# One ring of weight tiles for all stages, and the additions after a down pass in two groups

## The chip, the cores and the metric

The kernel runs on one core of a Trainium2 chip. The metric is the device time of one execution in microseconds; the median of three runs is what is compared.

## The reference

A decoder trunk of two layers over a sequence of 512 tokens of width 1024, in float32. Each layer is a token mixer followed by a gated feed-forward block with a causal convolution of width 3; every part reads an RMS-normed input and adds its result to the residual stream.

```
for i in range(2):
    h = rms_norm(x, norm_mix[i])
    x = x + (mixer_a(h, ...) if i == 0 else mixer_b(h, ...))
    h = rms_norm(x, norm_ffn[i])
    up = causal_dwconv(h @ w_up, conv_w, conv_b)      # 1024 -> 6144
    gate, val = jnp.split(up, 2, axis=-1)
    x = x + (gelu(gate) * val) @ w_down               # 3072 -> 1024
return rms_norm(x, norm_final)
```

Mixer A projects to 4096, mixes tokens in chunks of 128 and projects back; mixer B projects to 3072, convolves, runs a linear recurrence and projects back.

## The kernel before

**Numbers as pairs.** Activations lie transposed, features on the partitions, 128 to a tile. Every float32 operand of a matmul is kept as a high part and a low part of a faster type (`hi`, `lo`). For a weight chunk, `split` (line 94) makes them: ACT casts the raw chunk to `hi` (line 98) and DVE subtracts to get `lo` (line 99). Three matmuls, hi·hi, hi·lo and lo·hi, stand for one product.

**Weight chunks.** `load` (line 102) issues the DMA of a raw chunk of 128x1024 on SP's queue and then splits it. `block` (line 115) is the plain projection: per chunk of weights it does 24 matmuls of 512 columns into four PSUM banks, and at given chunks it calls hooks; `norm_stat` and `norm_spread` (lines 228 and 235) are such hooks, which turn the sum of squares `acc` into the factor of the norm by a few matmuls (`st`, `rb`).

**Stages.** The kernel has four stages: mixer A, the feed-forward of layer 0, mixer B, the feed-forward of layer 1. `enter` opens the pools of a stage and their memory is used again by the next. The tiles of raw, high and low weights come from the pool `wp` of the stage: three of each tag in the mixers, four high and four low ones in `conv_ffn` (line 522), where raw has three (line 103).

**End of a mixer.** `project` (line 257) multiplies by the output weights in two halves of four banks (`aop`, `bop` in the rows). For each of its banks it adds to the residual tile `xs[k]` (line 262), makes the normed input `xh`, `xl` of the next stage (line 209) and squares for the next norm (line 214).

**Feed-forward.** `up` (line 529) makes 256 gate and 256 value features at a time in 12 calls (`q`), each a `block` of four chunks (`fu`), followed by a scaling, the convolution, the GELU and the product. The down projection is written as a Strassen product with seven terms in `seven` (line 504): per `q`, `weight_sums` (line 469) makes two pairs of high and low parts, a and b, with three sums on DVE, two casts on ACT and two subtractions on DVE; then come 42 matmuls of 256 columns into seven banks, 18 with part a and 24 with part b. `down` (line 561) does this for two halves `m` of the outputs over six `q`. In the rows, `d000`, `d001` are the two halves of the first pass, `d060`, `d061` those of the second, `d100`, `d101` those of layer 1. The last part of layer 1 is a plain projection.

**After each half of a down pass** the seven banks are added to the residual (lines 567 to 580): one copy on ACT and eleven additions on DVE, all at high priority, seven of them with a PSUM operand:

```
nc.vector.tensor_tensor(x2[:, :, t1], x2[:, :, t1], banks[5], op=ALU.subtract)
nc.vector.tensor_tensor(x1[:, :, t1], banks[5], x1[:, :, t1], op=ALU.add)
nc.vector.tensor_tensor(x1[:, :, t1], banks[3], x1[:, :, t1], op=ALU.add)
```

`next_norm` (line 584) then makes the normed input of mixer B in the second pass of layer 0.

**What sets the order.** A scheduler orders each engine's instructions by priority and by when it believes their operands and memory free; splits and additions at `HIGH` go first. Each engine then runs its list strictly in order, and an instruction that waits holds up those behind it. A weight tile is free for its next use when the last matmul on it has ended.

Of the kernel before, what the change touches and what calls it, by code (L numbers as in the profile page):

```python
# [8 lines left out]
F32 = mybir.dt.float32  # L9
BF16 = mybir.dt.bfloat16  # L10
F32R = mybir.dt.float32r
AF = mybir.ActivationFunctionType
ALU = mybir.AluOpType

P = 128
S = 512
# [4 lines left out]
AG = 8  # L21
# [23 lines left out]
def trunk(ctx: ExitStack, tc: tile.TileContext, xT, vecs, a_w_in, a_w_sT, a_b_s, a_w_out,  # L45
          b_w_in, b_w_a, b_w_x, b_w_out, f_w_up, f_w_down, out):
    nc = tc.nc

    const = ctx.enter_context(tc.tile_pool(name="const", bufs=1))
    pp = ctx.enter_context(tc.tile_pool(name="pp", bufs=8, space=bass.MemoryType.PSUM))  # L50

    def psum(name="ps"):
# [39 lines left out]


    def split(raw, shape, name):
        hi = phase["wp"].tile(shape, F32R, tag="hi", name=f"{name}h")
        lo = phase["wp"].tile(shape, F32R, tag="lo", name=f"{name}l")
        with tc.high_priority(HIGH):
            nc.scalar.copy(hi, raw)
            nc.vector.tensor_tensor(lo, raw, hi.bitcast(F32), op=ALU.subtract)
        return hi, lo  # L100

    def load(shape, parts, name):
        raw = phase["wp"].tile(shape, F32, tag="raw", name=f"{name}r", bufs=3)
        for sl, src in parts:
            nc.sync.dma_start(sl(raw), src)
        return split(raw, shape, name)
# [39 lines left out]
    def load_x(k):  # L146
        nc.sync.dma_start(xs[k], xT[k * P:(k + 1) * P, :])

    mixer = enter(("wp", 3), ("yp", 24), ("wk", 7), ("bs", 1))
    bs = phase["bs"].tile([P, AG, P], F32, name="bs")  # L150


# [191 lines left out]
    wv = a_w_in.rearrange("(k p) n -> p k n", p=P)  # L344

    def first_chunk(kc, src):
        raw, hi, lo = (phase["wp"].tile([P, 2, 512], dt, tag=t, name=f"av0{kc}{t}") for t, dt in (("raw", F32), ("hi", F32R), ("lo", F32R)))
        for i in range(2):
            k = 2 * kc + i
            load_x(k)  # L350
            nc.sync.dma_start(raw[:, i], src[:, i])
            with tc.high_priority(HIGH):
                norm_input(k, g0[:, k:k + 1])
                nc.scalar.copy(hi[:, i], raw[:, i])
                nc.vector.tensor_tensor(lo[:, i], raw[:, i], hi[:, i].bitcast(F32), op=ALU.subtract)
        return hi, lo
# [43 lines left out]
            vparts[c, fb] = (h, l)  # L400


    wsr = phase["wp"].tile([P, AG, P], F32, tag="raw", name="wsr")
    nc.sync.dma_start(wsr, a_w_sT.rearrange("g s t -> s g t"))
    wsparts = []
    for i in range(AG // 2):
# [60 lines left out]


    def weight_sums(src, name):
        raw = phase["wp"].tile([P, 4, 256], F32, tag="raw", name=f"{name}r", bufs=3)  # L470
        for k in range(2):
            nc.sync.dma_start(raw[:, 2 * k:2 * k + 2], src[:, k])
        sums = phase["sm"].tile([P, 4, 256], F32, tag="sm", name=f"{name}s")
        parts = []
        with tc.high_priority(HIGH):
            nc.vector.tensor_tensor(sums[:, 0:2], raw[:, 1:3], raw[:, 0:1].broadcast_to([P, 2, 256]), op=ALU.add)
            nc.vector.tensor_tensor(sums[:, 2], raw[:, 1], sums[:, 1], op=ALU.add)
            nc.vector.tensor_tensor(sums[:, 3], raw[:, 3], sums[:, 2], op=ALU.add)
            for t, src in (("a", raw[:, 1:4]), ("b", sums)):
                n = src.shape[1]  # L480
                hi, lo = (phase["wp"].tile([P, n, 256], F32R, tag=g, name=f"{name}{t}{g}", padded_shape=[P, 4, 256]) for g in ("hi", "lo"))
                nc.scalar.copy(hi, src)
                nc.vector.tensor_tensor(lo, src, hi.bitcast(F32), op=ALU.subtract)
                parts.append((hi, lo))
        return parts
# [29 lines left out]
                                         stop=last and j == 1 and m == 2, skip_group_check=True)  # L515
        return banks

    def etile(name):
        return phase["wk"].tile([P, 2, HS], F32, tag="w", name=name)

    def conv_ffn(l, gain_name, gain_off, chunks):
        stack = enter(("wp", 4), ("y", 6), ("yr", 1), ("sm", 1), ("wk", 5))
        wu = f_w_up[l].rearrange("(k p) (two n) -> p k two n", p=P, two=2)
        wd = f_w_down[l].rearrange("(k p) (two n) -> p k two n", p=P, two=2)
        ys, plain = {}, []
        summed = NF // 2 if gain_name else NF // 4


        def up(q):
            def ld(kc):  # L530
                hi, lo = load([P, 2, 2, 256], [
                    (lambda t, h=h: t[:, :, h, :], wu[:, 2 * kc:2 * kc + 2, h, q * 256:(q + 1) * 256]) for h in range(2)
                ], f"fu{l}{q}{kc}")
                return hi.rearrange("p k h n -> p k (h n)"), lo.rearrange("p k h n -> p k (h n)")
            pss = block(KD, ld, xparts, f"f{q}", norm_hooks if q == 0 else {}, chunks)
            y = phase["y"].tile([P, 7, S], F32R, tag="y", name=f"y{q}")
            if q < summed:
                raw = phase["yr"].tile([P, 8, HS], F32, tag="yr", name=f"yr{q}")
            for j in range(2):
                ts = []  # L540
                for half in range(2):
                    f = half * NF + 2 * q + j
                    upt = work("up")
                    nc.vector.tensor_tensor(upt, pss[2 * half + j], rbc, op=ALU.mult)  # L544
                    t = work("cv")
                    conv(t, upt, 3, "f_conv_w", "f_conv_b", l * 6 * NF + f, 2 * NF, l * 2 * NF + f)
                    ts.append(t)
                nc.scalar.activation(ts[0], ts[0], AF.Gelu_apprx_tanh)  # L548
                if q < summed:
                    nc.vector.tensor_tensor(places(raw)[j], halves(ts[0]), halves(ts[1]), op=ALU.mult)  # L550
                else:
                    nc.vector.tensor_tensor(ts[1], ts[0], ts[1], op=ALU.mult)  # L552
                    h, lo = y[:, 2 * j], y[:, 2 * j + 1]
                    nc.scalar.copy(h, ts[1])  # L554
                    nc.vector.tensor_tensor(lo, ts[1], h.bitcast(F32), op=ALU.subtract)
                    plain.append((h, lo))
            if q < summed:
                input_sums(raw, y)
                ys[q] = y

        def down(qs, then):
            for m in range(2):
                banks = seven([(q, ys[q]) for q in qs],
                              lambda q: wd[:, 2 * q:2 * q + 2, :, m * 256:(m + 1) * 256], f"d{l}{qs[0]}{m}")
                x2, x1 = xall[:, 2 * m:2 * m + 2, :], xall[:, 4 + 2 * m:6 + 2 * m, :]
                t0, t1 = slice(0, HS), slice(HS, S)
                with tc.high_priority(HIGH):
                    e1, u2, u3 = (etile(f"d{qs[0]}{m}{t}") for t in ("e1", "u2", "u3"))
                    nc.scalar.copy(e1, banks[1])
                    nc.vector.tensor_tensor(x1[:, :, t0], banks[2], x1[:, :, t0], op=ALU.add)  # L570
                    nc.vector.tensor_tensor(x2[:, :, t0], x2[:, :, t0], banks[4], op=ALU.subtract)
                    nc.vector.tensor_tensor(u2, banks[6], e1, op=ALU.subtract)
                    nc.vector.tensor_tensor(u3, u2, banks[7], op=ALU.subtract)
                    nc.vector.tensor_tensor(x2[:, :, t1], x2[:, :, t1], banks[5], op=ALU.subtract)
                    nc.vector.tensor_tensor(x1[:, :, t1], banks[5], x1[:, :, t1], op=ALU.add)
                    nc.vector.tensor_tensor(x1[:, :, t1], banks[3], x1[:, :, t1], op=ALU.add)
                    for t in (t0, t1):
                        nc.vector.tensor_tensor(x2[:, :, t], x2[:, :, t], u3, op=ALU.add)
                    nc.vector.tensor_tensor(x1[:, :, t0], x1[:, :, t0], e1, op=ALU.add)
                    nc.vector.tensor_tensor(x1[:, :, t1], x1[:, :, t1], u2, op=ALU.subtract)  # L580
                if then:
                    then(m)

        def next_norm(m):
            for k in (2 * m, 2 * m + 1, 4 + 2 * m, 5 + 2 * m):
                norm_input(k, col(gain_name, gain_off + k))
                square(k)

        half = NF // 4
        for q in range(half + 1):  # L590
            up(q)
        down(list(range(half)), None)
        for q in range(half + 1, NF // 2):
            up(q)
        if gain_name:
            down(list(range(half, NF // 2)), next_norm)
        else:
            project_out(NF // 2, f_w_down[l][half * 256:, :], plain, f"fd{l}")
        stack.close()

    mixer.close()
    conv_ffn(0, "norm_mix", KD, None)
    mixer = enter(("wp", 3), ("yp", 24), ("wk", 7))
    log_sigmoid()


# [145 lines left out]
```

## Time and profile before

| | |
|---|---|
| median of 3 runs | 1365.67 us (1365.33 to 1366.09) |
| the profiled execution | 1364.13 us, of which the span is 1362.4 us |
| granted TensorE clock, mean | 0.989 |
| PE busy | 1327.4 us, 97% of the span |
| DVE, ACT busy | 956.7 us (70%), 591.0 us (43%) |
| DMA | 129.30 MB, mean 95 GB/s |

Times in rows are microseconds from the start of the span. In a timeline row the columns are start, length, engine, line, operation, output<-inputs, shape and count; in square brackets stand the idle time ahead of it and what ended it. A matmul's length is modelled and runs over the start of the next one; start to start is what counts. In a row of windows the columns are the stretch, its length, the busy time and the number of instructions of each of PE, PEld, DVE, ACT and POOL, the granted clock as a share of full speed, the share of DMA time and GB/s. A row of waits has the engine and line that waited, for what, the total in us, how many times, and the longest.

### The profile page before, as it was taken

The numbers are of one execution on the slowest core, as the hardware profiler recorded it, in microseconds if no ns is written. First come the engines' busy times: TensorE is split into PE (matmuls) and PEld (weight loads), VectorE is DVE, ScalarE is ACT, GpSimd is POOL, SyncE is SP. The second block draws the span as 40 slices with busy tenths as digits, with TensorE's granted clock in tenths as the row PEclk, the third lists the DMA queues.
The fourth block names the chain that finished last, engine by engine and source line by source line (L and its number), as shares of the span: only waits on it lengthen the run. The fifth ranks groups of instructions, "written<-read, shape, count | busy, mean of one in ns | idle before, by whom it ended". The sixth has DMA issues, their size and how long they took to land.

```text
span 1362.4 us, 16705 instructions
## 1 busy us (share of the span) xinstructions
PE 1327.4 (97%) x6510; PEld 1108.9 (81%) x6510; DVE 956.7 (70%) x1342; ACT 591.0 (43%) x767; POOL 12.1 (1%) x20
## 2 busy tenths in 40 slices
PE   9999999989999989999889999998999999999997
PEld 7888888868888988888878888886888889888886
DVE  7228765446878886778986799954677788675734
ACT  6455332333444433444443578633344443343432
POOL 1010000000000000000000000000000000000000
PEclk9999999999999999999889999998999999999998
DMA  6333222232232233222233333232323222422221
GB/s 227 95 98 103 84 82 78 92 103 93 93 98 88 68 93 124 94 92 77 69 103 94 93 93 93 93 108 74 97 93 96 90 78 89 130 94 96 94 72 62
DMA packets 106127, 129.30 MB, mean 95 GB/s; under 512 B 6464, under 2 KB 80192, under 8 KB 106048
## 3 DMA queue, kind: packets, MB, share of 16 engines
q1 hardware_dynamic: 105904, 128.23, 29.4%
q8 instruction: 51, 0.84, 0.2%
q14 instruction: 28, 0.23, 0.1%
q10 hardware_dynamic: 144, 0.00, 0.0%
HBM read 126.11 MB, written 2.10 MB: 94 GB/s over the span
## 4 chain that ended last, share of the span: by engine, by line
PE 90%; DVE 6%; issue 2%; ACT 1%; DVEq 0%; POOLq 0%; POOL 0%; ACTq 0%
PE f L110 13%; PE f L112 13%; PE f L111 13%; PE v L373 2%; PE u L110 2%; PE v L374 2%; PE u L112 2%; PE u L111 2%; PE d061m L514 2%; PE v L375 2%; PE aop L110 2%; PE aop L111 2%; PE aop L112 2%; PE d001m L514 2%; PE bx L110 2%
## 5 line engine op out<-in xcount | busy, mean ns | idle before, releaser
L457 DVE SCALAR_TENSOR_TENSOR cv<-up,vt,cv 128x511 f32<-128x511 f32 (+1 forms) x192 | 140.5, 745 | 24.4 <-ACT cv L455 23.1
L455 ACT ACTIVATE cv<-up,vt 128x512 f32<-128x512 f32 x96 | 77.4, 811 | 72.8 <-DVE up L544 72.8
L544 DVE TENSOR_TENSOR up<-f,rbc 128x512 f32<-128x512 f32 x96 | 65.1, 682 | 0.0
L548 ACT ACTIVATE cv<-cv 128x512 f32<-128x512 f32 x48 | 30.2, 629 | 45.5 <-DVE cv L457 45.0
L494 DVE TENSOR_TENSOR y<-yr,y 128x1792 fp32r<-128x1792 f32 x18 | 36.4, 2024 | 5.7 <-ACT y L493 5.7
L210 ACT ACTIVATE xh<-xall,vt 128x512 fp32r<-128x512 f32 x24 | 17.2, 716 | 48.6 <-DVE xall L262 35.7
L493 ACT CAST y<-yr 128x1792 fp32r<-128x1792 f32 x18 | 30.4, 1690 | 5.5 <-PE d001m L514 5.5
L433 DVE SCALAR_TENSOR_TENSOR sv<-sv,vt,bs 128x256 f32<-128x256 f32 x32 | 14.9, 477 | 19.1 <-PE sv L430 19.1
L219 ACT ACTIVATE sq<-xall 128x512 f32<-128x512 f32 (+1 forms) x37 | 21.7, 586 | 15.2 <-DVE xall L274 15.2
L457 DVE SCALAR_TENSOR_TENSOR xb<-xr,vt,xb 128x511 f32<-128x511 f32 (+2 forms) x36 | 25.5, 743 | 0.1
L550 DVE TENSOR_TENSOR yr<-cv 128x512 f32<-128x512 f32 x36 | 24.7, 686 | 0.6
L220 DVE TENSOR_TENSOR acc<-acc,sq 128x512 f32<-128x512 f32 (+1 forms) x37 | 23.7, 641 | 2.0 <-ACT sq L219 1.9
L554 ACT CAST y<-cv 128x512 fp32r<-128x512 f32 x12 | 7.3, 620 | 29.3 <-DVE cv L552 23.6
L211 DVE SCALAR_TENSOR_TENSOR xl<-xall,vt,xh 128x512 fp32r<-128x512 f32 x24 | 17.9, 745 | 2.3 <-ACT xh L210 2.2
L225 POOL TENSOR_TENSOR rc<-ms,mhalf 128x4 f32<-128x4 f32 (+1 forms) x6 | 5.4, 906 | 1256.0 <-DVE ms L224 1256.0
L429 PE MATMUL sv<-ws,vh 128*128 128x256 f32 x64 | 15.4, 324 | 0.0
L435 DVE SCALAR_TENSOR_TENSOR sv<-sv,vt 128x256 f32<-128x256 f32 x32 | 15.0, 479 | 0.4
L430 PE MATMUL sv<-ws,vl 128*128 128x128 f32 x64 | 14.2, 222 | 0.0
L682 DVE TENSOR_TENSOR_SCAN hs<-riyh,sq 128x512 f32<-128x512 f32 x12 | 14.0, 1202 | 0.0
L262 DVE TENSOR_TENSOR xall<-aop,xall 128x512 f32<-128x512 f32 x8 | 5.4, 685 | 10.9 <-PE aop L112 10.8
L262 DVE TENSOR_TENSOR xall<-bop,xall 128x512 f32<-128x512 f32 x8 | 5.4, 685 | 10.8 <-PE bop L112 10.8
L85 ACT ACT_TABLE_LOAD x10 | 12.8, 1283 | 0.1
(2573 smaller groups left out, 4500.3 us busy)
## 6 DMA issues: line engine op xcount, KB each, us to landing
xall<-xT SPq DMA_DIRECT2D x8, 256.0 KB, 5.6
outT<-o SPq DMA_DIRECT2D x8, 256.0 KB, 2.2
av00raw<-a_w_in SPq DMA_DIRECT2D x2, 256.0 KB, 3.7
av01raw<-a_w_in SPq DMA_DIRECT2D x2, 256.0 KB, 5.7
av02raw<-a_w_in SPq DMA_DIRECT2D x2, 256.0 KB, 6.3
av03raw<-a_w_in SPq DMA_DIRECT2D x2, 256.0 KB, 5.5
bs<-a_b_s SPq DMA_DIRECT2D x1, 512.0 KB, 6.0
av10r<-a_w_in SPq DMA_DIRECT2D x1, 512.0 KB, 6.7
```

Source lines behind the costliest of these rows:

```text
L110: nc.tensor.matmul(ps, wh, xh, start=first, stop=False)
L111: nc.tensor.matmul(ps, wh, xl, start=False, stop=False)
L112: nc.tensor.matmul(ps, wl, xh, start=False, stop=last)
L373: nc.tensor.matmul(pss[c], xh[kk][:, ts], hi[:, k, :], start=kk == 0, stop=False)
L374: nc.tensor.matmul(pss[c], xh[kk][:, ts], lo[:, k, :], start=False, stop=False)
L455: nc.scalar.activation(dst, src, AF.Identity, scale=col(wname, woff + last * wstep), bias=col(cname, coff))
L457: nc.vector.scalar_tensor_tensor(dst[:, i:], src[:, :S - i], col(wname, woff + (last - i) * wstep), dst[:, i:], op0=ALU.mult, op1=ALU.add)
L493: nc.scalar.copy(hi, raw[:, 0:7])
L494: nc.vector.tensor_tensor(lo, raw[:, 0:7], hi.bitcast(F32), op=ALU.subtract)
L514: nc.tensor.matmul(banks[b][:, j], wt[:, w, js], xt, start=first and j == 0 and m == 0, stop=last and j == 1 and m == 2, skip_group_check= ...
L544: nc.vector.tensor_tensor(upt, pss[2 * half + j], rbc, op=ALU.mult)
L548: nc.scalar.activation(ts[0], ts[0], AF.Gelu_apprx_tanh)
```

## The change

The pool `wp` is opened once for the whole kernel, with three tiles a tag, and all stages draw from it in turn; the stages' own pools go, and with them the fourth high and low tile of `conv_ffn`. The three temporaries of a down pass's end come from a pool `ev` of their own (`e`, `u`) in place of the work pool `wk`. The seven reads of PSUM that the additions had on DVE become five, and a second copy on ACT takes bank 5 out; only these, with both copies, are at high priority. The sums that only read SBUF follow at normal priority: one of 128x1024 and four of 128x2x256.

```diff
+    wp = ctx.enter_context(tc.tile_pool(name="wp", bufs=3))
...
-        hi = phase["wp"].tile(shape, F32R, tag="hi", name=f"{name}h")
-        lo = phase["wp"].tile(shape, F32R, tag="lo", name=f"{name}l")
+        hi = wp.tile(shape, F32R, tag="hi", name=f"{name}h")
+        lo = wp.tile(shape, F32R, tag="lo", name=f"{name}l")
...
-        raw = phase["wp"].tile(shape, F32, tag="raw", name=f"{name}r", bufs=3)
+        raw = wp.tile(shape, F32, tag="raw", name=f"{name}r")
...
-    mixer = enter(("wp", 3), ("yp", 24), ("wk", 7), ("bs", 1))
+    mixer = enter(("yp", 24), ("wk", 7), ("bs", 1))
...
-        stack = enter(("wp", 4), ("y", 6), ("yr", 1), ("sm", 1), ("wk", 5))
+        stack = enter(("y", 6), ("yr", 1), ("sm", 1), ("ev", 1), ("wk", 5))
...
+                e = phase["ev"].tile([P, 2, S], F32, tag="e", name=f"e{l}{qs[0]}{m}")
+                u = phase["ev"].tile([P, 2, S], F32, tag="u", name=f"u{l}{qs[0]}{m}")
                 with tc.high_priority(HIGH):
-                    e1, u2, u3 = (etile(f"d{qs[0]}{m}{t}") for t in ("e1", "u2", "u3"))
-                    nc.scalar.copy(e1, banks[1])
+                    nc.scalar.copy(e[:, :, t0], banks[1])
                     nc.vector.tensor_tensor(x1[:, :, t0], banks[2], x1[:, :, t0], op=ALU.add)
                     nc.vector.tensor_tensor(x2[:, :, t0], x2[:, :, t0], banks[4], op=ALU.subtract)
-                    nc.vector.tensor_tensor(u2, banks[6], e1, op=ALU.subtract)
-                    nc.vector.tensor_tensor(u3, u2, banks[7], op=ALU.subtract)
-                    nc.vector.tensor_tensor(x2[:, :, t1], x2[:, :, t1], banks[5], op=ALU.subtract)
-                    nc.vector.tensor_tensor(x1[:, :, t1], banks[5], x1[:, :, t1], op=ALU.add)
+                    nc.vector.tensor_tensor(u[:, :, t0], banks[6], e[:, :, t0], op=ALU.subtract)
+                    nc.vector.tensor_tensor(u[:, :, t1], u[:, :, t0], banks[7], op=ALU.subtract)
+                    nc.scalar.copy(e[:, :, t1], banks[5])
                     nc.vector.tensor_tensor(x1[:, :, t1], banks[3], x1[:, :, t1], op=ALU.add)
-                    for t in (t0, t1):
-                        nc.vector.tensor_tensor(x2[:, :, t], x2[:, :, t], u3, op=ALU.add)
-                    nc.vector.tensor_tensor(x1[:, :, t0], x1[:, :, t0], e1, op=ALU.add)
-                    nc.vector.tensor_tensor(x1[:, :, t1], x1[:, :, t1], u2, op=ALU.subtract)
+                nc.vector.tensor_tensor(x1, x1, e, op=ALU.add)
+                nc.vector.tensor_tensor(x1[:, :, t1], x1[:, :, t1], u[:, :, t0], op=ALU.subtract)
+                for t in (t0, t1):
+                    nc.vector.tensor_tensor(x2[:, :, t], x2[:, :, t], u[:, :, t1], op=ALU.add)
+                nc.vector.tensor_tensor(x2[:, :, t1], x2[:, :, t1], e[:, :, t1], op=ALU.subtract)
```

The orders of SP and POOL are as before. PE's differs in one place: the sums of squares for mixer B's norm (`st`) come 14 rows later, inside the third weight chunk, 15 matmuls into it and 9 ahead of `rb`. Line numbers of the changed kernel are one higher from line 50 on and shift again in `down`.

ACT where mixer A ends and the feed-forward of layer 0 begins, before (`aow` are chunks of mixer A's output weights, `fu` of the up projection, `xh` the normed residual, `sq` its squares):

```order
L98 CAST aow17h<-aow17r 128x1024
L210 ACTIVATE xh_67<-xall,vt 128x512
L219 ACTIVATE sq<-xall 128x512
L210 ACTIVATE xh_68<-xall,vt 128x512
L219 ACTIVATE sq<-xall 128x512
L210 ACTIVATE xh_69<-xall,vt 128x512
L219 ACTIVATE sq<-xall 128x512
L210 ACTIVATE xh_70<-xall,vt 128x512
L219 ACTIVATE sq<-xall 128x512
L98 CAST fu000h<-fu000r 128x1024
```

and the same place in the changed kernel:

```order
L99 CAST aow17h<-aow17r 128x1024
L99 CAST fu000h<-fu000r 128x1024
L99 CAST fu001h<-fu001r 128x1024
L211 ACTIVATE xh_70<-xall,vt 128x512
L220 ACTIVATE sq<-xall 128x512
L211 ACTIVATE xh_71<-xall,vt 128x512
L220 ACTIVATE sq<-xall 128x512
L99 CAST fu002h<-fu002r 128x1024
```

The first two casts of the new stage move from behind all eight instructions on the last residual tiles to a place ahead of them; the place from mixer B to layer 1 has the same shape.

ACT where the feed-forward of layer 0 ends and mixer B begins, before (`bx` are weight chunks of mixer B, wanted in the order bx00, bx02, bx01, bx03):

```order
L210 ACTIVATE xh_65<-xall,vt 128x512
L98 CAST bx00h<-bx00r 128x1024
L219 ACTIVATE sq<-xall 128x512
L98 CAST bx02h<-bx02r 128x1024
L210 ACTIVATE xh_66<-xall,vt 128x512
L98 CAST bx01h<-bx01r 128x1024
L219 ACTIVATE sq<-xall 128x512
L210 ACTIVATE xh_69<-xall,vt 128x512
L219 ACTIVATE sq<-xall 128x512
L210 ACTIVATE xh_70<-xall,vt 128x512
L219 ACTIVATE sq<-xall 128x512
L98 CAST bx03h<-bx03r 128x1024
```

and in the changed kernel:

```order
L99 CAST bx00h<-bx00r 128x1024
L568 COPY e_5709<-d061m_5360 128x2x256
L99 CAST bx02h<-bx02r 128x1024
L573 COPY e_5709<-d061m_5365 128x2x256
L99 CAST bx01h<-bx01r 128x1024
L99 CAST bx03h<-bx03r 128x1024
L211 ACTIVATE xh_72<-xall,vt 128x512
L211 ACTIVATE xh_68<-xall,vt 128x512
L220 ACTIVATE sq<-xall 128x512
L211 ACTIVATE xh_69<-xall,vt 128x512
L220 ACTIVATE sq<-xall 128x512 x2
L211 ACTIVATE xh_73<-xall,vt 128x512
```

All four casts of mixer B's first block now stand ahead of the normed inputs; the fourth one, bx03h, needs the tile that the matmuls on bx00 use.

DVE between the two halves of the second down pass, before (`blo` and `alo` are low parts of a weight pair, `s` its sums):

```order
L571 TENSOR_TENSOR xall<-xall,d060m_4984 128x2x256
L572 TENSOR_TENSOR d60u_5332<-d060m_4985,d60e_5331 128x512
L579 TENSOR_TENSOR xall<-xall,d60e_5331 128x2x256
L573 TENSOR_TENSOR d60u_5333<-d60u_5332,d060m_4986 128x512
L574 TENSOR_TENSOR xall<-xall,d060m_4987 128x2x256
L575 TENSOR_TENSOR xall<-d060m_4987,xall 128x2x256
L578 TENSOR_TENSOR xall<-xall,d60u_5333 128x2x256
L576 TENSOR_TENSOR xall<-d060m_4988,xall 128x2x256
L578 TENSOR_TENSOR xall<-xall,d60u_5333 128x2x256
L580 TENSOR_TENSOR xall<-xall,d60u_5332 128x2x256
L476 TENSOR_TENSOR d0616s<-d0616r 128x512
L483 TENSOR_TENSOR d0616alo<-d0616r,d0616ahi 128x768
```

and in the changed kernel:

```order
L484 TENSOR_TENSOR d06011blo<-d06011s,d06011bhi 128x1024
L569 TENSOR_TENSOR xall<-d060m_4980,xall 128x2x256
L570 TENSOR_TENSOR xall<-xall,d060m_4981 128x2x256
L477 TENSOR_TENSOR d0616s<-d0616r 128x512
L571 TENSOR_TENSOR u_5329<-d060m_4982,e_5328 128x2x256
L478 TENSOR_TENSOR d0616s<-d0616r,d0616s 128x256
L572 TENSOR_TENSOR u_5329<-u_5329,d060m_4983 128x2x256
L574 TENSOR_TENSOR xall<-d060m_4985,xall 128x2x256
L479 TENSOR_TENSOR d0616s<-d0616r,d0616s 128x256
L484 TENSOR_TENSOR d0616alo<-d0616r,d0616ahi 128x768
L575 TENSOR_TENSOR xall<-xall,e_5328 128x1024
L484 TENSOR_TENSOR d0616blo<-d0616s,d0616bhi 128x1024
```

The low part that the next half starts with now follows five additions and three sums, not eleven additions and one; the SBUF sums come between the following weight parts.

## Rows read from the trace of the kernel before

**Rows 1.** The page, part 1: busy time, share, instructions of PE.

```profile
PE 1327.4 (97%) x6510; PEld 1108.9 (81%) x6510; DVE 956.7 (70%) x1342; ACT 591.0 (43%) x767; POOL 12.1 (1%) x20
```

**Rows 2.** The waits of PE, longest first.

```profile
PE d061m L514 <- DVE d0616alo L483: 5.0, 1, 5.0
PE bx L110 <- ACT bx00h L98: 4.6, 1, 4.6
PE f L110 <- ACT fu100h L98: 4.5, 1, 4.5
PE f L110 <- ACT fu000h L98: 4.5, 1, 4.5
PE d001m L514 <- DVE d0011blo L483: 2.5, 1, 2.5
...
PE d101m L514 <- DVE d1011blo L483: 1.2, 1, 1.2
PE d101m L514 <- DVE d1011alo L483: 1.2, 1, 1.2
PE d001m L514 <- DVE d0010blo L483: 1.2, 1, 1.2
```

**Rows 3.** Timeline of PE at the three stage boundaries.

```profile
288.75 0.39 PE L112 MATMUL aop<-ay15h,aow17l 128*128 128x512 f32 x1
...
301.09 0.39 PE L110 MATMUL f<-xh,fu001h 128*128 128x512 f32 x1
...
306.71 0.95 PE L231 MATMUL st<-ones_f,acc 128*128 128x1 f32 x8
...
699.56 0.40 PE L514 MATMUL d061m<-y,d06111bhi 128*128 128x256 f32 x2
...
712.92 0.39 PE L110 MATMUL bx<-xh,bx02h 128*128 128x512 f32 x1
...
941.44 0.39 PE L112 MATMUL bop<-by11h,bow15l 128*128 128x512 f32 x1
...
954.97 0.40 PE L110 MATMUL f<-xh,fu101h 128*128 128x512 f32 x1
```

**Rows 4.** Windows: clock after waits, DVE in the second pass and in mixer B.

```profile
293.60:297.20 3.60, 3.49 (x8) 2.35 (x9) 3.54 (x4) 1.92 (x3) 0.00 (x0) 0.54 0.32 97
...
488.00:496.00 8.00, 5.50 (x42) 5.09 (x42) 7.03 (x10) 3.37 (x3) 0.00 (x0) 1.00 0.22 68
...
647.14:681.20 34.06, 29.10 (x222) 28.80 (x221) 31.14 (x48) 15.61 (x20) 0.00 (x0) 0.90 0.22 69
...
817.44:851.50 34.06, 34.06 (x148) 27.64 (x147) 34.06 (x50) 30.01 (x43) 0.00 (x0) 1.00 0.30 93
```

**Rows 5.** Timeline of PE in the down passes.

```profile
464.30 0.28 PE L514 MATMUL d000m<-y,d0002alo 128*128 128x256 f32 x1
...
469.34 0.28 PE L514 MATMUL d000m<-y,d0003alo 128*128 128x256 f32 x1
...
661.77 0.40 PE L514 MATMUL d060m<-y,d06011bhi 128*128 128x256 f32 x2
...
674.56 0.28 PE L514 MATMUL d061m<-y,d0617alo 128*128 128x256 f32 x1
```

**Rows 6.** Timeline of ACT and DVE: a cast, low parts, one addition.

```profile
292.59 1.03 ACT L98 CAST fu000h<-fu000r 128x1024 fp32r<-128x1024 f32 x1
...
455.27 1.23 DVE L483 TENSOR_TENSOR d0001blo<-d0001s,d0001bhi 128x1024 fp32r<-128x1024 f32 x1 [0.65 <-ACT d0001bhi L482]
...
663.72 0.68 DVE L576 TENSOR_TENSOR xall<-d060m,xall 128x512 f32<-128x512 f32 x1
...
681.34 0.95 DVE L483 TENSOR_TENSOR d0619alo<-d0619r,d0619ahi 128x768 fp32r<-128x768 f32 x1
...
686.14 0.95 DVE L483 TENSOR_TENSOR d06110alo<-d06110r,d06110ahi 128x768 fp32r<-128x768 f32 x1
```

More of the change, by code (lines that the diff above doesn't have):

```diff
@@ L346, in first_chunk @@
     def first_chunk(kc, src):
-        raw, hi, lo = (phase["wp"].tile([P, 2, 512], dt, tag=t, name=f"av0{kc}{t}") for t, dt in (("raw", F32), ("hi", F32R), ("lo", F32R)))
+        raw, hi, lo = (wp.tile([P, 2, 512], dt, tag=t, name=f"av0{kc}{t}") for t, dt in (("raw", F32), ("hi", F32R), ("lo", F32R)))
         for i in range(2):
@@ L400, in trunk @@
             vparts[c, fb] = (h, l)
-    wsr = phase["wp"].tile([P, AG, P], F32, tag="raw", name="wsr")
+    wsr = wp.tile([P, AG, P], F32, tag="raw", name="wsr")
     nc.sync.dma_start(wsr, a_w_sT.rearrange("g s t -> s g t"))
@@ L469, in weight_sums @@
     def weight_sums(src, name):
-        raw = phase["wp"].tile([P, 4, 256], F32, tag="raw", name=f"{name}r", bufs=3)
+        raw = wp.tile([P, 4, 256], F32, tag="raw", name=f"{name}r")
         for k in range(2):
@@ L480, in weight_sums @@
                 n = src.shape[1]
-                hi, lo = (phase["wp"].tile([P, n, 256], F32R, tag=g, name=f"{name}{t}{g}", padded_shape=[P, 4, 256]) for g in ("hi", "lo"))
+                hi, lo = (wp.tile([P, n, 256], F32R, tag=g, name=f"{name}{t}{g}", padded_shape=[P, 4, 256]) for g in ("hi", "lo"))
                 nc.scalar.copy(hi, src)
@@ L516, in seven @@
         return banks
-    def etile(name):
-        return phase["wk"].tile([P, 2, HS], F32, tag="w", name=name)
     def conv_ffn(l, gain_name, gain_off, chunks):
-        stack = enter(("wp", 4), ("y", 6), ("yr", 1), ("sm", 1), ("wk", 5))
+        stack = enter(("y", 6), ("yr", 1), ("sm", 1), ("ev", 1), ("wk", 5))
         wu = f_w_up[l].rearrange("(k p) (two n) -> p k two n", p=P, two=2)
@@ L602, in trunk @@
     conv_ffn(0, "norm_mix", KD, None)
-    mixer = enter(("wp", 3), ("yp", 24), ("wk", 7))
+    mixer = enter(("yp", 24), ("wk", 7))
     log_sigmoid()
```

## The prediction

> **What bounds the kernel now.** I read the page first: PE is busy for 97% of the span [rows 1], so only what makes PE wait, or run slowly, can shorten this kernel. Then the waits of PE: eight places hold nearly all of its idle time inside the span, and each waits for a high or low part of weights [rows 2]. Three of them, 4.5, 4.6 and 4.5 us, are stage boundaries (mixer A to layer 0's feed-forward, that to mixer B, mixer B to layer 1). The other five lie where one half of a down pass gives way to the next: 1.2 and 2.5 us in d001, 5.0 us in d061, twice 1.2 us in d101.
>
> Third, the timeline of PE, because idle time is not the whole price. A chunk of 24 matmuls takes 306.71 - 301.09 = 5.62 us at full clock [rows 3]. The last matmul of mixer A starts at 288.75 and lasts 0.23 us; the second chunk of the next stage starts at 301.09. Between lie 12.1 us for 5.6 us of work: 6.5 us lost, of which 4.5 us are the wait. The rest is a slow start: in the stretch behind the wait the granted clock is 0.54 of full [rows 4]. By the same sum the boundary to mixer B loses 712.92 - 699.80 - 5.62 = 7.5 us and the one to layer 1 954.97 - 941.67 - 5.62 = 7.7 us [rows 3]. In the down passes a pair of weight parts is 5.04 us of matmuls [rows 5]; d061 reaches its second pair at 674.56, 12.55 us after d060's end at 662.01, so 7.5 us are lost there too, while the shorter waits of d001 (3.7 us) and d101 (2.4 us) leave the clock at 1.00 [rows 4]. In all 35 us.
>
> Fourth, DVE: in the window over d060 and d061 it is busy for 31.1 of 34.1 us [rows 4]. There PE waits for DVE's amount of work, not for one late instruction.
>
> **The change, part by part.**
>
> *Loads across a stage boundary.* Before, the first weights of a stage are cast after all eight ACT instructions on the last residual tiles: fu000h starts at 292.59, 3.6 us after PE went idle [rows 6]. With one ring the first two casts stand ahead of those. The tile of fu000 is the one that aow15 leaves, two chunks (11 us) before PE needs it, and a split is a cast of 1.03 and a subtraction of 1.23 us [rows 6]. The four banks that it wants were emptied half a projection earlier. The first two chunks also need only normed tiles 0 to 3, made during the second half of the projection; tiles 4 to 7 are wanted 11 us after the boundary, and their additions, normed parts and squares take some 7 us of DVE. So both waits into a feed-forward go, with their slow starts: 6.5 + 7.7 = 14.2 us. Nothing new is late there.
>
> *Into mixer B.* The wait of 7.5 us goes in the same way, but here the change adds a wait. Cast bx03h needs the tile of bx00, which PE leaves 5.6 us after the boundary, and it stands on ACT ahead of the normed inputs and squares of four tiles. Counted along DVE from there (bx03l, four low parts, four sums of squares, bx10l in between, which waits for bx02's end at 11.2 us), the sum of squares is done about 14.9 us after the boundary. PE comes to `st` at 11.2 us and 15 matmuls more, 14.7 us, and to `rb` only nine matmuls (2.1 us) behind; the factor and the two diagonals need about 3 us. I take 1.5 us lost, between nothing and a whole chunk, 5.6 us. Boundaries together: 21.7 - 1.5 = 20.2 us gained.
>
> *The additions.* Eleven of 0.68 us [rows 6] become nine of 0.68 and one of 128x1024 (1.23 us as the low parts of that width): 7.5 against 7.35 us of DVE, six times. In amount that is nothing. The second copy on ACT is at most a cast of 1.03 us on an engine with 57% idle. What moves is their order: in d061 the first low part now follows one PSUM addition, one sum and itself (0.7 + 0.4 + 0.95), about 2 us after PE's end instead of 5. But what is put off falls between the next pairs' parts, on an engine that is full there [rows 4], and PE then waits for part b of the next pairs in place of part a of the first. I count the order as zero; bounds: 5.5 us gained in d061 (3 us of wait, 2.5 us of slow clock), 2 us lost.
>
> *Three tiles in place of four.* Between pairs without other work DVE makes a pair in 686.14 - 681.34 = 4.80 us against PE's 5.04 [rows 5, 6], so it can hardly catch up within a pass, and what it is ahead at the start is what it lives on. Before, d0001b was ready at 456.50 [rows 6] and wanted at 464.30 - 24 x 0.12 = 461.42 [rows 5]: 4.9 us ahead. With three tiles a part b may be cast only when PE has ended part a of the pair before, 5.04 us ahead of need; less 2.26 us for cast and subtraction, 2.8 us are the most. Up to 2.1 us of lead go, in each of three passes (d00, d06, d10). Following the changed row lists of DVE and ACT through the three passes with these durations, I find some 1.8, 1.1 and 1.0 us more waiting; I take 3.9 us lost, between 0 and 6.3. In the up calls three tiles cost nothing: there the lead is two chunks (11 us), and mixer B runs on three tiles with DVE busy in 34.06 of 34.06 us and PE as well [rows 4].
>
> *The sum.* 20.2 - 3.9 = 16.3 us, from the profiled execution's 1364.1 us to 1347.8 us. The median of the runs stands 1.5 us above that execution: **1349.4 us**.
>
> **Rivals.**
>
> *The grouping pays (0.12).* The banks free sooner, the put-off sums find idle time after all, and d061's restart 2 us after its end keeps the clock up. For it: the wait of d061 is for one low part behind eleven additions [rows 2]. Against it: DVE's 31.1 of 34.1 us [rows 4]. Without the 3.9 us lost and with 5.5 us gained in d061: 1340 us.
>
> *The clock falls in the down passes (0.13).* Waits of 1.2 and 2.5 us kept the clock, those from 4.5 us on lost it [rows 2, 4]; I expect waits of 2 to 3 us, several to a pass. If each of three joints falls to half clock, at d061's price of 7.5 - 5.0 = 2.5 us: 1357 us; with a fourth in d060, where I expect 2.6 us, 1359.5 us. The Trainium skill ("TensorE: Matmul & The Clock Gate", HAM oscillation) says that a kernel whose PE waits again and again between bursts pays a cold start after each; by that rule the time would be this rival's. The trace agrees for the long waits only.
>
> *Three tiles starve the down passes: slower (0.05).* There are 36 pairs (six `q`, two halves, three passes), and spare time is only 0.24 us a pair [rows 5, 6]. If the wait of a cast for PE's last use of the tile puts 0.8 us in series with each pair's preparation, 29 us are lost, 1378 us; from 0.45 us a pair on (16.3 / 36) the change is a loss. Against it: the way from a freed tile to a finished part b is cast, subtraction, three sums, cast, subtraction, about 6 us, with 7.2 us to go. The Trainium skill ("Perfetto Trace Analysis", Optimization Strategy) reads a gap that repeats for a stretch on the engine that should be full as a sign of too few buffers; by that rule fewer tiles go the wrong way, and the time is this rival's. The window of mixer B, on three tiles, shows no such gap [rows 4].
>
> *No change (0.04).* The casts come early but PE still waits at the boundaries, for a bank or for a normed tile: then 1366 us. The order lists and the banks speak against it.
>
> **How the numbers follow.** My forecast has 0.66, and for it alone I expect 1345 to 1355 us (boundaries 1 us better to 4 worse, passes 4 better to 2.4 worse, not all at once). To leave out no more than 2 in 10 the range goes from the first rival's 1340 to 1358 us, inside the second's. A difference of 0.2% (2.7 us) is about what measurement can tell from none. Faster takes the forecast and the two rivals below 1360 us, 0.91; same 0.04; slower 0.05.
>
> **What would show it.** In the profile of the changed kernel PE's waits for fu000h, bx00h and fu100h are gone, the second chunks start within 6 us of the boundaries, and the clock there stays at 1.00. PE shows a wait of 1 to 2 us at `st` or `rb` of mixer B. In d00, d06 and d10 waits for `blo` parts of 1 to 3 us stand in several places, DVE almost without a gap beside them. I am wrong if d061 has no waits after its first pair, if the half-speed stretches move into the down passes, or if the up calls show PE waiting for `fu` parts.

## The result, and the profile after

The changed kernel takes **1344.62 us** (median of 4 runs, 1344.57 to 1345.26), the kernel before beside it 1365.50 us: a ratio of 0.985 (0.983 to 0.987), 20.9 us less. The prediction was 1349.4 us, with a range of 1340 to 1358. The profiled execution took 1344.57 us, its span 1342.8 us, against 1364.13 and 1362.4 us before; its mean granted clock is 0.997 against 0.989. One execution of a kernel below, early_pair, took 2824.76 us, twice the others, and is left out of its median.

The page of the changed kernel, part 1, answers to [rows 1]; PE does the same matmuls in 8.1 us less, since fewer of them run at a lowered clock:

```profile
PE 1319.3 (98%) x6510; PEld 1103.8 (82%) x6510; DVE 955.9 (71%) x1336; ACT 595.2 (44%) x773; POOL 12.0 (1%) x20
```

The waits of PE in the changed kernel, longest first, answer to [rows 2]:

```profile
PE d001m L515 <- DVE d0011blo L484: 2.6, 1, 2.6
PE d001m L515 <- DVE d0010blo L484: 2.5, 1, 2.5
PE d061m L515 <- DVE d0616alo L484: 2.0, 1, 2.0
PE d060m L515 <- DVE d06010blo L484: 1.9, 1, 1.9
PE d101m L515 <- DVE d1011blo L484: 1.6, 1, 1.6
...
PE d101m L515 <- DVE d1010blo L484: 1.1, 1, 1.1
...
PE d061m L515 <- DVE d0618blo L484: 0.9, 1, 0.9
PE d061m L515 <- DVE d0619blo L484: 0.5, 1, 0.5
PE d061m L515 <- DVE d0617blo L484: 0.4, 1, 0.4
```

The three waits of a stage's start, for fu000h, bx00h and fu100h, are gone. Apart from 3.8 us at the first and the last matmuls of the kernel, as before, what is left stands in the down passes, 13.5 us in nine waits, and eight of the nine are for part b.

The timeline of PE at the first two boundaries and at `st` of mixer B, changed kernel, answers to [rows 3]:

```profile
288.29 0.39 PE L113 MATMUL aop<-ay15h,aow17l 128*128 128x512 f32 x1
...
294.14 0.39 PE L111 MATMUL f<-xh,fu001h 128*128 128x512 f32 x1
...
694.50 0.40 PE L515 MATMUL d061m<-y,d06111bhi 128*128 128x256 f32 x2
694.74 0.39 PE L111 MATMUL bx<-xh,bx00h 128*128 128x512 f32 x1
...
700.35 0.39 PE L111 MATMUL bx<-xh,bx02h 128*128 128x512 f32 x1
...
709.27 0.95 PE L232 MATMUL st<-ones_f,acc 128*128 128x1 f32 x8
```

From the start of mixer A's last matmul to that of the second chunk it is 5.85 us, a chunk (5.62) and one matmul (0.23): nothing is lost. Into mixer B the last pair of matmuls gives way at 694.74 without a gap and the second chunk starts 5.61 us later.

Windows of the changed kernel (columns as in [rows 4]): the boundaries to layer 0's feed-forward and to mixer B, then two stretches of d001, each behind one of its two waits:

```profile
288.00:306.00 18.00, 18.00 (x83) 14.67 (x82) 10.39 (x17) 5.92 (x8) 1.01 (x1) 1.00 0.22 70
...
699.00:714.00 15.00, 14.90 (x67) 11.68 (x66) 11.89 (x20) 7.94 (x12) 1.01 (x1) 1.00 0.33 102
...
482.40:489.00 6.60, 6.60 (x42) 6.48 (x42) 4.31 (x8) 2.29 (x2) 0.00 (x0) 0.74 0.30 89
491.70:494.00 2.30, 2.30 (x19) 2.30 (x20) 2.21 (x4) 0.00 (x0) 0.00 (x0) 1.00 0.00 0
```

At the boundaries the clock is whole now. In d001 it fell once: 42 matmuls took 6.60 us where a pair takes 5.04 [rows 5], 1.6 us lost, behind a wait of 2.5 us; behind the next wait, of 2.6 us, it stayed at 1.00. The 0.74 is a mean: from 484 to 487 us the granted clock was 0.50, the lower of its two levels (1.2 GHz).

The lengths of six stretches, each from the start of one named matmul to that of another in the profiled executions, tell where the time went (us). The last four columns are kernels of the next section:

| stretch | before | changed | three_tiles | ring_only | one_group | late_y_early_pair |
|---|---|---|---|---|---|---|
| last on aow17l to first on d0000alo | 165.5 | 159.0 | 165.6 | 159.0 | 159.0 | 159.0 |
| d00: d0000alo to fu070h | 65.0 | 67.5 | 67.8 | 67.8 | 67.7 | 62.9 |
| d06 and boundary: d0606alo to bx02h | 81.3 | 73.1 | 82.4 | 75.2 | 76.5 | 72.2 |
| mixer B: bx02h to last on bow15l | 228.5 | 229.2 | 228.6 | 229.1 | 229.0 | 229.2 |
| boundary: bow15l to fu101h | 13.5 | 5.8 | 13.3 | 5.8 | 5.8 | 5.8 |
| d10: d1000alo to fu170h | 63.4 | 63.9 | 65.9 | 65.9 | 64.4 | 62.6 |

### The profile page after: what moved, and what is told of

Same layout as the page of the kernel before. It is cut to its first block, busy times and chain, and to the rows that moved or that the text cites. A ratio compares the mean times of both kernels' runs of the same rounds, so it can differ in the third digit from the quotient of the medians.

```text
span 1342.8 us, 16731 instructions
## 1 busy us (share of the span) xinstructions
PE 1319.3 (98%) x6510; PEld 1103.8 (82%) x6510; DVE 955.9 (71%) x1336; ACT 595.2 (44%) x773; POOL 12.0 (1%) x20
## 4 chain that ended last, share of the span: by engine, by line
PE 90%; DVE 7%; issue 2%; ACT 1%; DVEq 0%; POOLq 0%; POOL 0%; ACTq 0%
PE f L111 13%; PE f L112 13%; PE f L113 13%; PE u L111 2%; PE v L374 2%; PE v L375 2%; PE u L113 2%; PE u L112 2%; PE v L376 2%; PE aop L111 2%; PE aop L113 2%; PE aop L112 2%; PE d001m L515 2%; PE d101m L515 2%; PE bx L113 2%
## 5 line engine op out<-in xcount | busy, mean ns | idle before, releaser
L431 PE MATMUL sv<-ws,vl 128*128 128x128 f32 x64 | 14.2, 222 | 0.0
L490 DVE TENSOR_TENSOR yr<-yr 128x512 f32<-128x512 f32 x18 | 12.5, 692 | 0.6
L431 PEld LDWEIGHTS sv<-ws,vl 128*128 128x128 f32 x64 | 12.2, 191 | 0.5
```

## The experiments

Each says what it changes against the kernel before or the changed one. Times are medians, with the kernel before on the same chip at 1365.96 us in the first two sets and 1366.84 us in the third.

**Ring, tiles and grouping apart.** The first kernel, ring_only, is the changed one with the old additions:

```diff
-        stack = enter(("y", 6), ("yr", 1), ("sm", 1), ("ev", 1), ("wk", 5))
+        stack = enter(("y", 6), ("yr", 1), ("sm", 1), ("wk", 5))
...
-                    nc.scalar.copy(e[:, :, t0], banks[1])
+                    e1, u2, u3 = (etile(f"d{qs[0]}{m}{t}") for t in ("e1", "u2", "u3"))
+                    nc.scalar.copy(e1, banks[1])
...
```

> The changed kernel with one ring of three weight tiles, but with the additions at the end of each half of a down pass as before the change: one copy, eleven additions, all at high priority, temporaries from the work pool. Theory (the ring makes the gain, the grouping is neutral): the waits at fu000h, bx00h and fu100h are gone, d061's wait for d0616alo is back at 4 to 6 us, and the time is 1345 to 1350 us. Rival (the grouping carries much of it): 1352 us or more, with the extra waits inside d00, d06 and d10.

It took 1349.56 us (1348.94 to 1349.65), ratio 0.988 (0.987 to 0.989). Its waits of PE:

```profile
PE d061m L515 <- DVE d0616alo L484: 5.1, 1, 5.1
PE d001m L515 <- DVE d0010blo L484: 2.6, 1, 2.6
PE d001m L515 <- DVE d0011blo L484: 2.5, 1, 2.5
PE d101m L515 <- DVE d1010blo L484: 2.2, 1, 2.2
```

The ring with three tiles alone gives, by the median, what the whole change had been forecast to give. d061's wait is back, as expected. Behind it, and in d10 behind d1010blo, the clock fell:

```profile
660.00:668.00 8.00, 2.89 (x17) 2.69 (x16) 8.00 (x14) 4.05 (x7) 0.00 (x0) 0.87 0.03 8
...
1127.00:1133.00 6.00, 6.00 (x39) 5.82 (x38) 4.47 (x8) 2.09 (x4) 0.00 (x0) 0.74 0.19 61
```

In the changed kernel it stayed whole at both places:

```profile
660.00:668.00 8.00, 6.29 (x51) 6.17 (x52) 8.00 (x13) 3.74 (x5) 0.00 (x0) 1.00 0.22 69
...
1122.00:1129.00 7.00, 5.27 (x42) 5.09 (x42) 6.93 (x11) 2.82 (x4) 0.00 (x0) 1.00 0.36 106
```

The second, three_tiles, is the kernel before with a shorter pool:

```diff
-        stack = enter(("wp", 4), ("y", 6), ("yr", 1), ("sm", 1), ("wk", 5))
+        stack = enter(("wp", 3), ("y", 6), ("yr", 1), ("sm", 1), ("wk", 5))
```

> The kernel before with three weight tiles of each tag in the feed-forward in place of four, nothing else. Theory (three tiles cost some us in the passes d00, d06, d10): the three boundary waits stay at 4.5 us each, PE waits longer for low parts of part b, and the time is 1367 to 1371 us (forecast of the cost: 3.9 us, bounds 0 to 6.3). Rival 1 (three tiles cost nothing): 1365 to 1366 us with the same list of waits. Rival 2 (three tiles starve the passes): over 1375 us.

It took 1372.5 us (1370.1 to 1375.9), ratio 1.005 (1.004 to 1.007): 6.5 us slower, over the 1367 to 1371 that was expected, far from starving. Its waits in the passes, and two windows of d001 and d101:

```profile
PE d061m L514 <- DVE d0616alo L483: 5.1, 1, 5.1
...
PE d001m L514 <- DVE d0010blo L483: 2.6, 1, 2.6
PE d001m L514 <- DVE d0011blo L483: 2.5, 1, 2.5
PE d101m L514 <- DVE d1010blo L483: 2.2, 1, 2.2
PE d060m L514 <- DVE d06010blo L483: 1.9, 1, 1.9
...
PE d101m L514 <- DVE d1011blo L483: 1.3, 1, 1.3
```

```profile
496.00:502.00 6.00, 4.44 (x24) 4.44 (x25) 4.74 (x7) 1.05 (x1) 0.00 (x0) 0.72 0.20 67
...
1148.00:1154.00 6.00, 5.56 (x37) 5.35 (x36) 4.42 (x8) 2.56 (x4) 0.00 (x0) 0.79 0.27 87
```

The waits of the passes d00, d06 and d10 rise from 3.7, 5.0 and 2.4 us [rows 2] to 5.1, 7.0 and 3.5 us, 4.5 us of the 6.0 by which this profiled execution (1370.1 us) is longer. By the stretches d00 and d10 grew by 1.5 and 1.4 us more than their waits, with a clock that fell behind these (0.72 and 0.79 above), and d06 by 0.9 us less. The other five executions took 1370.6 to 1375.9 us, at a mean granted clock of 0.985 to 0.983 against 0.986.

From three_tiles to ring_only the ring stands alone: 22.9 us by the medians, 20.5 by the profiled executions.

The third, three_tiles_grouped, adds the change's additions (`e` and `u`, two groups) to three_tiles:

> The kernel before with three weight tiles in the feed-forward and with the additions in two groups as after the change; each stage still has a pool of its own. Against the run with three tiles alone this is the grouping alone. Theory (grouping is neutral to a few us better, through d061's restart): 0 to 4 us less than the kernel with three tiles alone, 1364 to 1369 us, the boundary waits unchanged at 4.5 us. Rival (the grouping carries much of the gain): 8 us less or more than three tiles alone, 1360 us or less.

It took 1369.53 us (1368.51 to 1371.12), ratio 1.003 (1.002 to 1.004): 3.0 us less than three_tiles, a difference inside the theory, though the time is 0.5 us above its 1369. On the ring the same grouping is worth 1349.56 - 1344.62 = 4.9 us.

The fourth, one_group, asks what of the grouping does it. It is the changed kernel with its own sums, of which the five on SBUF stand at high priority too:

```diff
-                nc.vector.tensor_tensor(x1, x1, e, op=ALU.add)
+                    nc.vector.tensor_tensor(x1, x1, e, op=ALU.add)
...
-                nc.vector.tensor_tensor(x2[:, :, t1], x2[:, :, t1], e[:, :, t1], op=ALU.subtract)
+                    nc.vector.tensor_tensor(x2[:, :, t1], x2[:, :, t1], e[:, :, t1], op=ALU.subtract)
```

> The changed kernel, with its own ten sums at the end of a half (wider forms, second copy on ACT and all), but the five that only read SBUF at high priority too, so that they stand in one group again. Theory (the grouping's 5 us come from the order, which lets the low part of d0616a go ahead of the SBUF sums): PE's wait for d0616alo goes from 2.0 back to 4 to 5.5 us and the slow start behind it returns, the short waits inside d061 (0.9 + 0.5 + 0.4 us) go in part, and the time is 1346 to 1350 us. Rival (the gain comes from fewer and wider sums and from the second copy on ACT): 1344 to 1345.5 us.

It took 1350.21 us (1348.71 to 1350.65), 0.2 us above the theory's 1350 and no better than ring_only. Its first wait, and its clock behind it:

```profile
PE d061m L515 <- DVE d0616alo L484: 5.5, 1, 5.5
```

```profile
667.00:673.00 6.00, 6.00 (x36) 6.00 (x35) 6.00 (x10) 4.15 (x7) 0.00 (x0) 0.64 0.44 131
```

So in the sum the worth of the grouping is the order: fewer reads of PSUM, a wider sum and a second copy on ACT give nothing by themselves. That is shown for d061: with the same operations on DVE, d06 and its boundary take 76.5 us in one group and 73.1 in two. In d10 it is not: there one_group has 1.5 of the 2.0 us that the changed kernel has over ring_only (64.4 and 63.9 against 65.9), though its wait for d1010blo is 2.1 us, mostly since the clock, which fell behind 2.2 us in ring_only, stayed whole. Whether the additions' form or chance kept it up stays open.

**What is left in the passes.** The first try, late_y6, writes the sums, cast and low part of call 6's product tile `y` behind the first down pass (`up` returns them as a function that is called after `down`):

```diff
+                if q == NF // 4:
+                    return lambda: input_sums(raw, y)
                 input_sums(raw, y)
```

> The changed kernel with one step moved: the sums of the product tile y of up call 6, which make its cast and its low part (about 2 us of DVE), are written behind the first down pass, and so no longer stand ahead of d0011blo on DVE. Theory (PE waits in d00 for the amount of DVE work ahead of blo parts): the wait of 2.6 us for d0011blo shrinks by 1.5 to 2.6 us and the time is 1342 to 1344 us. Rival (the wait has another cause, or what is put off falls on the next call): within 1 us of the changed kernel, 1344 to 1346 us.

It took 1345.48 us (1345.26 to 1347.77): a miss, and the trace of ACT says why. The cast stands where it stood, 5.79 us of waiting for PE and all, with d0011bhi behind it:

```profile
480.42 0.83 ACT L483 CAST d0011ahi<-d0011r 128x768 fp32r<-128x768 f32 x1
487.03 1.69 ACT L494 CAST y<-yr 128x1792 fp32r<-128x1792 f32 x1 [5.79 <-PE d001m L515]
488.63 1.04 ACT L483 CAST d0011bhi<-d0011s 128x1024 fp32r<-128x1024 f32 x1
```

The scheduler fills a gap with whatever it believes ready; a later place in the program doesn't keep it out. So late_y_queued ties the cast behind another one on ACT (`cast[0]` is the last part-b cast):

```diff
+            if n == at and later:
+                with tc.issue_after(cast[0].ins):
+                    while later:
+                        later.pop(0)()
```

> The changed kernel, with the cast and the low part of the product tile of up call 6 (both layers) queued on ACT behind the last part-b cast of the first pass, and those of up call 11 of layer 0 queued behind the cast of d06010b in place of ahead of it. This time the place in ACT's list does move (the kernel late_y6 left it where it was, since the scheduler still filled ACT's gap with that cast). Theory (the waits left at d0011blo, d1011blo and d06010blo come from one cast of y that sits ahead of the part-b cast in ACT's list and waits there for PE, and from its 2 us low part on DVE): these three waits, 2.6 + 1.6 + 1.9 us, fall to under 0.7 us each, a new one of up to 1.2 us may stand at d06011blo, and the time is 1338.5 to 1342 us. Rival (DVE's amount of work or the three tiles make these waits): they move to other pairs of the same passes and the time stays at 1343 us or more.

It took 1340.09 us (1339.95 to 1340.75), 4.5 us less than the changed kernel. Of its waits of PE:

```profile
PE d001m L523 <- DVE d0010blo L486: 2.5, 1, 2.5
PE d061m L523 <- DVE d0616alo L486: 1.6, 1, 1.6
...
PE d060m L523 <- DVE d06011blo L486: 1.2, 1, 1.2
...
PE d101m L523 <- DVE d1011blo L486: 1.0, 1, 1.0
```

d0011blo is gone from the list, d06010blo has become the 1.2 us at d06011blo, and d1011blo went from 1.6 to 1.0 us, less than expected. That call 6's cast and low part, which nobody needed so soon, made the wait for d0011blo is shown; the other two waits, once theirs were moved, fell by 0.7 and 0.6 us only. The run moves cast and low part together and doesn't tell them apart. In the changed kernel both stood in the way: DVE sat idle for the cast, and then did the low part ahead of d0011blo.

```profile
488.43 2.03 DVE L495 TENSOR_TENSOR y<-yr,y 128x1792 fp32r<-128x1792 f32 x1 [2.29 <-ACT y L494]
490.37 1.22 DVE L484 TENSOR_TENSOR d0011blo<-d0011s,d0011bhi 128x1024 fp32r<-128x1024 f32 x1
```

The next, early_pair, writes the first weight pair of the second half ahead of the additions:

```diff
+                if m == 0:
+                    given = weight_sums(weight(1)(qs[0]), f"d{l}{qs[0]}1{qs[0]}")
```

> The changed kernel, with the first weight pair of the second half of each down pass (its three sums, casts and low parts) written ahead of the additions that end the first half, in place of behind them. Theory (what is left at the joint of the two halves is order on DVE, not amount): the waits for d0010blo (2.5 us), d0616alo (2.0 us) and d1010blo (1.1 us) lose 2 to 5 us in all, PE gets no new wait for a bank, and the time is 1339.5 to 1342.5 us. Rival (the additions that are pushed back now hold the banks, or DVE's amount of work decides and the waits move to the pairs behind): 1343.5 to 1346 us.

It took 1342.56 us (1342.54 to 1343.60), 2.1 us less than the changed kernel: 0.06 us above the theory's range and below the rival's. d0010blo falls from 2.5 to 0.8 us, d0616alo from 2.0 to 0.6, and d1010blo is no longer among the waits of 0.5 us and more, but, as the rival said, waits move to the pairs behind: d0617blo rises from 0.4 to 1.5 us and d0011blo from 2.6 to 2.8.

> Both edits of the two runs before, on the changed kernel. Theory: they act at different places, so the gains add up: 1334 to 1339 us, with under 6 us of PE's waits left in the three passes (13.4 us in the changed kernel). Rival (both draw on the same DVE time): no better than the better one of the two by more than 1 us.

Both edits together took 1339.59 us (1339.49 to 1339.74): by the time the rival holds, only 0.5 us better than late_y_queued. Its waits in the passes are 7.6 us in all, where under 6 were expected. Of its waits of PE:

```profile
PE d061m L523 <- DVE d0617blo L486: 1.5, 1, 1.5
...
PE d060m L523 <- DVE d06011blo L486: 1.2, 1, 1.2
...
PE d061m L523 <- DVE d0618blo L486: 0.9, 1, 0.9
PE f L113 <- DVE fu070l L100: 0.8, 1, 0.8
```

In d061, where the changed kernel's DVE is busy for 29.7 of 33.0 us, what one pair gains the next pays. In d00 the two edits do add up, 1.8 us less than late_y_queued (62.9 against 64.7), but the up call behind it takes 1.1 us longer, with a new wait for fu070l. In the third set, beside one_group, the changed kernel and this one ran once more:

> The changed kernel itself, once more, on the same chip as the two beside it. Both theories: 1344 to 1346 us. What it is for: whether the granted clock falls at the same joints as in its first profile. If the fall behind a wait of about 2.5 us in d001 belongs to the kernel's order, it is there again at d0010blo; if it depends on when the wait falls, it may stand behind another wait of that length or be gone, and the runs scatter by about 2 us.

> The version with the casts of y queued behind part b and with the first pair of the second half written ahead of the additions, once more, beside the changed kernel on the same chip. Theory: 1339 to 1341 us, 4 to 6 us below the changed kernel. Rival (the difference seen before was one of chips or of a clock that fell once): within 2 us of it.

The changed kernel took 1345.14 us (1344.74 to 1346.81), ratio 0.985 (0.983 to 0.986), and late_y_early_pair 1339.39 us (1339.22 to 1340.58), ratio 0.980 (0.979 to 0.982): 5.8 us less, the fastest of all. In the changed kernel's second profile the clock fell at the same joint, 0.74 in 482.40:489.00, and nowhere else in the passes.

**Sums on GpSimd.** In sums_on_pool the five sums on SBUF of each half run there:

```diff
-                nc.vector.tensor_tensor(x1, x1, e, op=ALU.add)
+                nc.gpsimd.tensor_tensor(x1, x1, e, op=ALU.add)
...
```

> The changed kernel with the five additions of each half that only read SBUF on GpSimd in place of DVE. Theory (DVE's amount of work makes the short waits inside d061, 0.9 + 0.5 + 0.4 us, and part of the one at d0010blo): DVE is relieved of 3.7 us per half, these waits go, and the time is 1340 to 1343.5 us. Rival (GpSimd takes several times as long for a sum, or slows DVE beside it; the residual and with it the normed input of mixer B come late): a new wait at the start of mixer B or in d061 and 1345 us or more.

It took 1361.62 us (1360.94 to 1363.23), 17 us more than the changed kernel: the rival. DVE lost 30 instructions and yet is busy for 954.1 us (955.9 in the changed kernel). Its timeline beside GpSimd's sums, which run from 660.91 to 670.85, and PE's wait at `st` of mixer B:

```profile
662.37 2.01 DVE L484 TENSOR_TENSOR d0616alo<-d0616r,d0616ahi 128x768 fp32r<-128x768 f32 x1
664.31 3.41 DVE L484 TENSOR_TENSOR d0616blo<-d0616s,d0616bhi 128x1024 fp32r<-128x1024 f32 x1
...
675.72 0.95 DVE L484 TENSOR_TENSOR d0618alo<-d0618r,d0618ahi 128x768 fp32r<-128x768 f32 x1
```

```profile
716.23 1.84 PE L232 MATMUL st<-ones_f,acc 128*128 128x1 f32 x8 [4.34 <-DVE acc L221]
```

The same low part takes 2.01 us beside GpSimd and 0.95 us without it, the one of 1024 columns 3.41 against 1.23 us [rows 6].

## Why the prediction was right, point by point

**Loads across a boundary: right.** 6.5, 7.5 and 7.7 us were said to be lost, and the ring wins 6.5 us at the first boundary (165.5 to 159.0) and 7.7 at the third (13.5 to 5.8). At mixer B three_tiles against ring_only gives 82.4 - 75.2 = 7.2 us.

**The new wait into mixer B: there, but smaller.** The sum of squares was to be ready 14.9 us after the boundary and 1.5 us to be lost. In the changed kernel the boundary is at 694.74, its last addition starts at 708.24 and takes 0.68: 14.2 us. PE came to `st` at 709.27, 0.35 us later, and did not wait. Mixer B is 0.6 us longer than before, of which the trace shows 0.2 as a gap of PE ahead of `rb`. DVE's operations of 0.68 us started 0.60 us apart, which the count along DVE had not fully taken in. That this deadline is a real one shows in sums_on_pool: a late `acc` cost 4.3 us there.

**The additions: the step that failed.** "I count the order as zero" was wrong by 4.9 us on the ring (3.0 us without it), near the upper bound of 5.5, but not in the way of that bound, which had all of it in d061. From ring_only to the changed kernel it is 2.1 us in d06 and its boundary, 2.0 in d10, where I saw nothing to gain, and 0.3 in d00; another 0.6 us by which the two profiled executions differ lie in mixer A, ahead of anything that the grouping changes.

In d061 the mechanism named there was right: the wait for the first low part fell from 5.1 to 2.0 us and the clock stayed whole, and waits of 0.9, 0.5 and 0.4 us for the next pairs' part b came instead. The error was to take these as worth as much as what was saved. Saved were 3.1 us of wait and 1.8 us of slow start (in ring_only it is 32.0 us from d0616alo to bx00h, for six pairs of 5.04 us); 2.8 us came back (33.0 us in the changed kernel). Behind the zero stood the reading that PE waits there for DVE's amount of work; one_group, with the same operations, shows that their order alone is worth 3.4 us there. In d10 the wait for d1010blo fell from 2.2 to 1.1 us, that for d1011blo rose from 1.3 to 1.6, and the clock, which had fallen, stayed whole.

The rival "the grouping pays" had the size right, and d061's clock behind a restart of 2.0 us; the put-off sums did cost waits, and three tiles were not free.

**Three tiles: mis-sized.** 3.9 us were said, with a bound of 6.3; the runs show 6.5 by the medians, 6.0 by the profiled executions. The waits grew by 1.4, 2.0 and 1.1 us in d00, d06 and d10 (forecast 1.8, 1.1, 1.0), 4.5 us. The rest is the clock, which I had left to a rival.

**The sum.** By the profiled executions: three tiles +6.0 (1364.13 to 1370.1), the ring -20.5 (to 1349.58), the grouping -5.0 (to 1344.57). Forecast were +3.9, -20.2 and 0. Two errors of opposite sign left the forecast 3.2 us above the profiled execution (1347.8 against 1344.57); that it came so close is in part luck. The 1.5 us added for the median make it 4.8: in the changed kernel median and profiled execution are the same to 0.05 us.

**The clock in the passes: in part.** A stretch at 0.74 of full clock behind a 2.5 us wait costs 1.6 us in the changed kernel; the rival had three or four of them, at 2.5 us each. It stayed whole behind 2.6 us in d001 and 2.0 us in d061. Without the grouping, in ring_only, it fell in all three passes (0.72 in 490.00:496.00 of d001, and the two windows shown above). The Trainium skill ("TensorE: Matmul & The Clock Gate", HAM oscillation) has such a price after each wait for a kernel whose waits last longer than the matmuls between them, which these do not (2 to 3 us against pairs of 5.04 us); the runs bear it out for some of these waits only.

**Starving: no.** three_tiles is 6.5 us slower, not 29, and the up calls, on three tiles too, show no wait for `fu` parts in the changed kernel.

What wasn't tried: four tiles on the ring, and the cast of `y` moved without its low part.

## What to carry to other kernels

When stages draw from one ring, the first weights of a stage are ready before the last one ends, and the gain can be read beforehand: the wait of the bound engine, plus the slow start behind it. Where an in-order engine is full, split what must be done now (what frees the banks, what the next matmul needs) from what may wait, by priority; the same work in one group was worth nothing here in the sum. Look too for an instruction that waits at the head of an engine's list although nobody needs it soon: moving the casts and low parts of three calls gave 4.5 us more, and they had to be tied behind another instruction, since a later place in the program left one where it was.

## What the runs showed of the hardware that I had not expected

Sums on GpSimd slow DVE instead of relieving it: low parts of two SBUF operands took 2.01 and 3.41 us beside them against 0.95 and 1.23 us. The Trainium skill ("SBUF — State Buffer", SBUF: two separate sides) says that the two engines share a pair of ports under an exclusive lock, which a DVE operation with two SBUF inputs also takes against a GpSimd operation that reads SBUF. The trace agrees: between 660.91 and 670.85 all five DVE operations with two SBUF inputs grew (the shortest from 0.42 to 0.96 us), while the addition at 660.88, with one operand in PSUM, took 0.69 us as it does without them.

The clock's fall is no matter of a wait's length alone: it kept at 1.00 behind 2.5 us in d001 before [rows 2, 4] and behind 2.6 us in the changed kernel, and fell behind 2.5 us there and behind 1.9 us in d060 of late_y6, as its window shows:

```profile
651.00:657.00 6.00, 4.14 (x24) 3.94 (x23) 4.74 (x7) 1.83 (x3) 0.00 (x0) 0.74 0.18 56
```

That execution is 2.3 us above its kernel's median, at a mean granted clock of 0.994 against 0.995 to 0.997 in the other three, so one and the same program can go either way. Which of them falls stays open. In the changed kernel's d001 and here a fall cost 1.6 and 1.5 us.
